# Scores of the new pair ahead of the old pair's transposes in a woven two-layer encoder

## The chip, the cores and the metric

The kernel runs on one core of a Trainium2 chip. The core has five engines with queues of their own: PE (TensorE, matrix products and transposes into PSUM), DVE (VectorE), ACT (ScalarE), POOL (GpSimd) and SP (SyncE, which issues the DMAs here). Each takes its instructions in the order of its queue, and they wait for one another by semaphores. The metric is device time in microseconds (us) of one execution, smaller is better.

## What is computed

A two-layer encoder trunk on 512 frames of 1024 channels, fp32, batch 1. Cut to what matters here:

```python
h = x
for layer in range(2):
    xn = rms_norm(h, norm_mix_g[layer])
    if layer == 0:   # A: sparse attention, each query keeps the top 128 admissible keys (rotary, 8 heads)
                     # B: chunked attention with a learned relative bias (8 heads)
        mix = even_mixer(xn, ...)
    else:            # C: forgetting attention (8 heads); D: windowed grouped attention with sinks (rotary, 8 heads)
        mix = odd_mixer(xn, ...)
    h = h + mix      # both mixers end in one output projection of their two head groups
    h = h + conv_gated_ffn(rms_norm(h, norm_ffn_g[layer]), ...)
return rms_norm(h, norm_out_g)
```

Every attention is: scores q.k, a bias or mask, softmax over the keys, product with v.

## The kernel before

**Precision.** Each fp32 operand is split into a high and a low part, and each product is three matmuls (`mm3`, L175 to 178): high with high, high with low, low with high. `hilo` (L182) makes such a pair from a result in PSUM: ACT copies the high part (L183), DVE subtracts to get the low part (L184). Weights come through a stream (`Stream`, L118): SP issues a DMA into `raw` (two buffers), ACT makes `whi` (L136), DVE or, for some, POOL makes `wlo` (L138); four buffers each.

**PSUM banks.** There are eight: two with the tag `acc` for projections, four with the tag `s` for scores, two with the tag `tp` for transposes, for the attention's output and for one narrow block of the scores (L97). A bank is taken in turn and can be filled again once its last reader is done.

**Weaves.** Attention is done for pairs of heads, one pair after another. A call of `weave(prev, cur, fill, n)` (L513) does the scores and the softmax of the new pair `cur` and, woven into them, the transposes, the product with v and the storing of the old pair `prev`. Between these steps stand `n` steps of filling, cut into seven parts by the percentages in `PARTS`. A step is one `yield` of a projection: one `mm3` of 512 columns, three matmuls. The filling is a queue of projections in a fixed order: in layer 0 the q and k of later B pairs, then `A1` and `A2` (q and k of the A pairs, four pieces of 128 frames each, 8 steps a piece), with `vA` between them, then `oB`, the half of the output projection that belongs to B (8 chunks of 4 steps). The lists `FILL_B`, `FILL_A`, `FILL_C`, `FILL_D` give the `n` of each weave. I call the weaves B0 to B3, A0 to A4, C0 to C3, D0 to D4; A4 has no new pair.

**The start of a weave** before the change, in the order of the code:

- T0, `prev.turn(0, 0)`: four transposes of the old pair's head 0 into one `tp` bank (L480), emptied by `hilo` into `PTh` and `PTl`.
- The score, `cur.score()`: 24 products (L442) of 64 rows and 128 to 512 columns, in a fixed order. The block of row 1 of head 0 goes into one `tp` bank with the first products, that of head 1 into another `tp` bank with the last three; the other blocks go into the four `s` banks.
- R0 and R1, `cur.soft(e, (1,))` for heads 0 and 1: DVE adds the bias to that row block and takes its minimum (L463, tile `nm`), which frees the `tp` bank; ACT exponentiates (L465), DVE inverts the sum (L467), POOL scales.
- T1, `prev.turn(0, 1)`: four more transposes into a `tp` bank; then the first part of the filling, then T2, `prev.turn(0, 2)`, two transposes, and the rest of the softmax of head 0.

Later in the weave the old pair's products with v go into a `tp` bank and are stored by ACT (L506) and DVE (L507, tile `Y`).

**Rotary transposes.** When a piece of `A1` or `A2` ends, `evac_A` (L716) applies the rotary (three products on DVE at L363, a sum on POOL at L365) and hands four transposes with their evacuations, `turn` at L724 (PE L727), to `later` (L154). `later.push(n, fn)` runs `fn` after `n` ticks; a tick falls at the end of every piece of a projection.

**The end.** In the second layer's MLP the last of the eight chunks of the down projection is done in two halves of 256 columns (L848): each begins with `lead_sums` (L858), which adds up over partitions the squares that POOL has gathered from the first seven chunks (L213), two tiny products (L861, four matmuls on PE), and goes on with 66 matmuls (22 `mm3`).

The queues' orders are not quite that of the code: a planner goes through the instructions by their place in the code, with durations of its own, and lets a later one go first where an earlier one is not ready by its reckoning. The order of the score's products among themselves is fixed (L445).

Of the kernel before, what the change touches and what calls it, by code (L numbers as in the profile page):

```python
# [22 lines left out]
NFF = DFF // 128  # L23
# [51 lines left out]
NI = 324  # L75
ND = 264
FILL_B = (8, 24, 24, 24, 24)
FILL_A = (20, 22, 18, 12, 11)
FILL_C = (6, 18, 16, 15, 12)
FILL_D = (10, 9, 9, 9, 8)  # L80
PARTS = (0, 20, 40, 50, 60, 72, 90, 100)
# [5 lines left out]
def trunk(ctx, tc, a, out):  # L87
# [11 lines left out]
    def bank(tag, shape=(128, 512)):  # L99
        return psum.tile(list(shape), F32, name=tag, tag=tag, bufs=banks[tag])  # L100
# [72 lines left out]
    later = Later()  # L173

    def mm3(o, lh, ll, rh, rl, start, stop):  # L175
        nc.tensor.matmul(o, lh, rh, start=start, stop=False)  # L176
        nc.tensor.matmul(o, lh, rl, start=False, stop=False)  # L177
        nc.tensor.matmul(o, ll, rh, start=False, stop=stop)  # L178
# [80 lines left out]
    class Fill:  # L259
# [16 lines left out]
        def run(self):  # L276
            while self.q:
                self.step(1)
# [234 lines left out]
    def weave(prev, cur, fill, n, mid=None, share=PARTS):  # L513
        cut = [n * p // 100 for p in share]
        parts = [b - a for a, b in zip(cut, cut[1:])]
        if prev is not None:
            prev.turn(0, 0)
        if cur is not None:
            cur.score()
            for e in range(2):  # L520
                cur.begin(e)
                cur.soft(e, (1,))
        if prev is not None:
            prev.turn(0, 1)
        if cur is not None and cur.early:
            for e in range(2):
                cur.rest(e)
                cur.soft(e, (2, 0, 3))
        fill.step(parts[0])
        if prev is not None:  # L530
            prev.turn(0, 2)
        if cur is not None and not cur.early:
            cur.rest(0)
            cur.soft(0, (2, 0, 3))
        if prev is not None:
            prev.av(0, 0)
        fill.step(parts[1])
        if prev is not None:
            prev.av(0, 1)
            prev.store(0)  # L540
        if mid is not None:
            mid(0)
        fill.step(parts[2])
        if prev is not None:
            prev.turn(1, 0)
        fill.step(parts[3])
        if prev is not None:
            prev.turn(1, 1)
        fill.step(parts[4])
        if prev is not None:  # L550
            prev.turn(1, 2)
        if cur is not None and not cur.early:
            cur.rest(1)
            cur.soft(1, (2, 0, 3))
        if prev is not None:
            prev.av(1, 0)
        if mid is not None:
            mid(1)
        fill.step(parts[5])
        if prev is not None:  # L560
            prev.av(1, 1)
            prev.store(1)
        fill.step(parts[6])
# [41 lines left out]
    with ExitStack() as st:  # L605
# [110 lines left out]
        def evac_A(half):  # L716
            def f(t, o):
                if t == 0:
                    for p in range(2):
                        qkA[2 * half + p] = mp.tile([128, 2, 2, SEQ], F32R, name="qk", tag="qk", bufs=3)  # L720
                qr = sp.tile([128, 8, HD], F32, name="scr2", tag="scr2", bufs=2)
                rope(o.rearrange("p (a d) -> p a d", a=8), t, slice(0, 2), qr, 8)

                def turn():  # L724
                    pt = bank("tp", (128, 2, 2, 128))
                    for b in range(4):
                        nc.tensor.transpose(pt[:, b // 2, b % 2, :],  # L727
                                            qr[:, 2 * b:2 * b + 2].rearrange("p a d -> p (a d)"), ident)
                    for p in range(2):
                        qk = qkA[2 * half + p]  # L730
                        ts_ = slice(t * 128, (t + 1) * 128)
                        hilo(qk[:, 0, :, ts_], qk[:, 1, :, ts_], pt[:, :, p, :])
                later.push(1, turn)
            return f

        for f in chan_pair(mp, ("qB", 0), ("kB", 0), pairs[0]):
# [28 lines left out]
        for p in range(4):  # L765
# [4 lines left out]
            cur = Pair(mp, job, 2)  # L770
            weave(pend, cur, fill, FILL_A[p])
            if p == 0:
# [3 lines left out]
            pend = cur  # L776
        fill.add(out_half("oA", lambda k: pairs[4 + k]["y"], after=lambda c: absorb(c, 1), lead=(0, 1, 2)))
        weave(pend, None, fill, FILL_A[4])
        fill.run()

    def ffn(layer, after):
        with ExitStack() as st:
            fp = st.enter_context(tc.tile_pool(name=f"ffn{layer}", bufs=1))
            cw = fp.tile([128, 192], F32, name="cw")[:, :4 * NC_FF].rearrange("p (a b) -> p a b", b=4)
            nc.sync.dma_start(cw, a["conv"][layer])
            act = [fp.tile([128, 2, SEQ], F32R, name=f"act{j}") for j in range(NFF)]

            def conv(o, c, dst):
                v = fp.tile([128, SEQ], F32, name="ov", tag="ov", bufs=2)
                nc.vector.tensor_tensor(v, o, R, OP.mult)  # L790
                nc.scalar.activation(dst, v, AF.Identity, scale=cw[:, c, 2:3], bias=cw[:, c, 3:4])
                nc.vector.scalar_tensor_tensor(dst[:, 1:], v[:, :SEQ - 1], cw[:, c, 1:2], dst[:, 1:],
                                               op0=OP.mult, op1=OP.add)
                nc.vector.scalar_tensor_tensor(dst[:, 2:], v[:, :SEQ - 2], cw[:, c, 0:1], dst[:, 2:],
                                               op0=OP.mult, op1=OP.add)

            def up(key):
                W.ahead(2)
                ws = W.get(key, 128)
                o = bank("acc" if key[0] == "g" else "s")  # L800
                run(chan_mm(o, ws))
                return o

            def first_two():
                W.ahead(2)
                os_ = bank("acc"), bank("s")
                gens = [chan_mm(o, W.get((x, layer, 0), 128)) for x, o in zip("gu", os_)]
                for gen in gens:
                    for _ in range(KD - 2):
                        next(gen)  # L810
                for gen in gens:
                    run(gen)
                return os_

            for j in range(NFF):
                tmp = sp.tile([128, 2, SEQ], F32, name="scr", tag="scr")
                if j == 0:
                    g, u = first_two()
                    token_roots()
                    roots()  # L820
                else:
                    g = up(("g", layer, j))
                conv(g, j, tmp[:, 0])
                nc.scalar.activation(tmp[:, 0], tmp[:, 0], AF.Silu)
                if j > 0:
                    u = up(("u", layer, j))
                conv(u, NFF + j, tmp[:, 1])
                nc.vector.tensor_tensor(tmp[:, 0], tmp[:, 0], tmp[:, 1], OP.mult)  # L828
                hilo(act[j][:, 0], act[j][:, 1], tmp[:, 0])
            hold = [None]  # L830

            def weights(c, k):
                n = c * NFF + k
                if n % 8 == 0:
                    W.ahead(2)
                    hold[0] = W.get(("w", layer, n // 8), 128)
                return [x[:, n % 8, :] for x in hold[0]]

            for c in range(KD - 1 if layer else KD):
                o = bank("acc")  # L840
                for k in range(NFF):
                    wh, wl = weights(c, k)
                    mm3(o, wh, wl, act[k][:, 0], act[k][:, 1], k == 0, k == NFF - 1)
                add_resid(c, o)
                after(c, slice(0, SEQ))
            if layer:
                ws = [weights(KD - 1, k) for k in range(NFF)]
                for cols in (slice(0, 256), slice(256, 512)):  # L848
                    o = bank("acc")
                    lead_sums(cols)  # L850
                    for k in range(NFF):
                        mm3(o[:, cols], *ws[k], act[k][:, 0, cols], act[k][:, 1, cols], k == 0, k == NFF - 1)
                    add_resid(KD - 1, o, cols)
                    after(KD - 1, cols)
# [3 lines left out]
    def lead_sums(cols):  # L858
        pt = sums["t"] = bank("tp", (128, NT))
        for t in range(cols.start // 128, cols.stop // 128):  # L860
            nc.tensor.matmul(pt[:, t:t + 1], hold_ss["t"][:, t * 128:(t + 1) * 128], ones[:, 0:1],  # L861
                             start=t * 128 == cols.start, stop=False)
# [401 lines left out]
```

## Time and profile before

| | |
|---|---|
| median of 3 runs | 1233.71 us (1233.11 to 1233.74) |
| the profiled execution | 1234.3 us, span 1232.4 us |
| mean granted clock of PE | 0.996 |
| busy | PE 98%, DVE 66%, ACT 48%, POOL 16% of the span |

The span runs from the first to the last instruction; some 1.9 us lie around it. PE's busy time is the union of its matmuls' modelled durations, so 98% does not mean that PE is at its peak. Rows name a line of the program (L480), the tile written and the tiles read (`tp<-ident,P`), partitions by elements, and how many instructions are merged (x4).

### The profile page before, as it was taken

The numbers are of one execution on the slowest core, as the hardware profiler recorded it, in microseconds if no ns is written. First come the engines' busy times: TensorE is split into PE (matmuls) and PEld (weight loads), VectorE is DVE, ScalarE is ACT, GpSimd is POOL, SyncE is SP. The second block draws the span as 40 slices with busy tenths as digits, with TensorE's granted clock in tenths as the row PEclk, the third lists the DMA queues.
The fourth block names the chain that finished last, engine by engine and source line by source line (L and its number), as shares of the span: only waits on it lengthen the run. The fifth ranks groups of instructions, "written<-read, shape, count | busy, mean of one in ns | idle before, by whom it ended". The sixth has DMA issues, their size and how long they took to land.

```text
span 1232.4 us, 15886 instructions
## 1 busy us (share of the span) xinstructions
PE 1204.5 (98%) x5908; PEld 993.3 (81%) x5908; DVE 813.8 (66%) x1469; ACT 593.5 (48%) x1008; POOL 199.9 (16%) x275
## 2 busy tenths in 40 slices
PE   8999899999999999999999999999999999999997
PEld 7777788778888888888888878778888888888886
DVE  7988987778877777733325566897777777762222
ACT  6555565666444444432224577785544444442221
POOL 3365322212000000000111354322000000000000
PEclk9999999999999999999999999999999999999999
DMA  6232213313333233233222320122332333323321
GB/s 217 86 105 85 69 44 120 111 35 106 104 102 102 88 102 101 88 102 102 87 70 86 114 70 24 37 84 72 103 94 95 103 93 96 103 92 96 103 69 69
DMA packets 35373, 111.71 MB, mean 91 GB/s; under 512 B 4192, under 2 KB 6624, under 8 KB 35296
## 3 DMA queue, kind: packets, MB, share of 16 engines
q1 hardware_dynamic: 35296, 110.70, 28.7%
q8 instruction: 46, 0.75, 0.3%
q14 instruction: 31, 0.25, 0.1%
HBM read 108.59 MB, written 2.10 MB: 90 GB/s over the span
## 4 chain that ended last, share of the span: by engine, by line
PE 80%; DVE 8%; ACT 4%; issue 4%; DMA 2%; POOL 1%; POOLq 0%; SPq 0%; DVEq 0%; ACTq 0%
PE acc L176 17%; PE acc L178 17%; PE acc L177 17%; PE s L176 8%; PE s L177 8%; PE s L178 8%; PE tp L480 1%; DMA raw<-in_w 1%; DVE wlo L138 1%; DVE wk L682 1%; ACT whi L136 1%; DVE P L463 1%; DVE m L681 1%; ACT P L465 1%; PE tp L497 1%
## 5 line engine op out<-in xcount | busy, mean ns | idle before, releaser
L138 DVE TENSOR_TENSOR wlo<-raw,whi 128x1024 fp32r<-128x1024 f32 (+2 forms) x188 | 237.0, 1261 | 159.8 <-ACT whi L136 156.9
L136 ACT ACTIVATE whi<-raw 128x1024 fp32r<-128x1024 f32 (+2 forms) x196 | 204.4, 1044 | 217.3 <-PE acc L177 144.5
L176 PE MATMUL acc<-xT,whi 128*128 128x512 f32 x480 | 189.2, 394 | 0.0
L178 PE MATMUL acc<-xT,wlo 128*128 128x512 f32 x480 | 187.0, 390 | 0.0
L177 PE MATMUL acc<-xT,whi 128*128 128x512 f32 x480 | 187.0, 390 | 0.0
L213 POOL TENSOR_TENSOR scr<-scr,os 128x512 f32<-128x512 f32 x24 | 34.5, 1439 | 722.2 <-ACT os L211 722.2
L176 PE MATMUL acc<-act,whi 128*128 128x512 f32 (+1 forms) x374 | 140.9, 377 | 0.0
L177 PE MATMUL acc<-act,whi 128*128 128x512 f32 (+1 forms) x374 | 140.9, 377 | 0.0
L178 PE MATMUL acc<-act,wlo 128*128 128x512 f32 (+1 forms) x374 | 140.9, 377 | 0.0
L176 PE MATMUL s<-xT,whi 128*128 128x512 f32 x352 | 136.9, 389 | 0.0
L177 PE MATMUL s<-xT,whi 128*128 128x512 f32 x352 | 136.9, 389 | 0.0
L178 PE MATMUL s<-xT,wlo 128*128 128x512 f32 x352 | 136.9, 389 | 0.0
L178 PEld LDWEIGHTS acc<-xT,wlo 128*128 128x128 f32 x480 | 90.2, 188 | 19.0
L176 PEld LDWEIGHTS acc<-xT,whi 128*128 128x128 f32 x480 | 90.1, 188 | 19.0 <-issue 1.0
L177 PEld LDWEIGHTS acc<-xT,whi 128*128 128x128 f32 x480 | 90.1, 188 | 18.6 <-issue 0.5
L176 PE MATMUL acc<-whi,xT 128*128 128x512 f32 (+2 forms) x208 | 84.5, 408 | 1.4 <-ACT whi L136 1.2
L177 PE MATMUL acc<-wlo,xT 128*128 128x512 f32 (+2 forms) x208 | 81.3, 392 | 1.1 <-DVE wlo L138 1.1
L178 PE MATMUL acc<-whi,xT 128*128 128x512 f32 (+2 forms) x208 | 81.3, 392 | 0.5 <-DVE xT L231 0.5
L176 PEld LDWEIGHTS acc<-act,whi 128*128 128x128 f32 x374 | 70.4, 188 | 13.0
L183 ACT ACTIVATE act<-scr 128x512 fp32r<-128x512 f32 x44 | 27.7, 630 | 110.2 <-DVE scr L828 110.2
L177 PEld LDWEIGHTS acc<-act,whi 128*128 128x128 f32 x374 | 70.4, 188 | 12.9
L178 PEld LDWEIGHTS acc<-act,wlo 128*128 128x128 f32 x374 | 70.4, 188 | 12.8
(244 smaller groups left out, 2174.5 us busy)
## 6 DMA issues: line engine op xcount, KB each, us to landing
raw<-in_w SPq DMA_DIRECT2D x188, 512.0 KB, 3.5
h<-in_x SPq DMA_DIRECT2D x16, 256.0 KB, 4.7
T<-in_relb SPq DMA_DIRECT2D x8, 256.0 KB, 2.8
raw<-in_w_i SPq DMA_DIRECT2D x4, 324.0 KB, 3.9
raw<-in_w_d SPq DMA_DIRECT2D x4, 264.0 KB, 2.8
out_y<-h SPq DMA_DIRECT2D x4, 256.0 KB, 2.2
out_y<-h SPq DMA_DIRECT2D x2, 384.0 KB, 2.4
ropeC<-in_ropeC SPq DMA_DIRECT2D x2, 256.0 KB, 4.1
```

The source lines that it names most:

```text
L136: nc.scalar.activation(hi[:, :w], raw[:, :w], AF.Copy)
L138: eng.tensor_tensor(lo[:, :w], raw[:, :w], hi[:, :w].bitcast(F32), OP.subtract)
L176: nc.tensor.matmul(o, lh, rh, start=start, stop=False)
L177: nc.tensor.matmul(o, lh, rl, start=False, stop=False)
L178: nc.tensor.matmul(o, ll, rh, start=False, stop=stop)
L183: nc.scalar.activation(dh, src, AF.Copy)
L213: eng.tensor_tensor(ss, ss, sq, OP.add)
L463: nc.vector.tensor_tensor_reduce(out=L, in0=self.s[e][i], in1=self.job["bias"][e][i], scale=1.0, scalar=3e38, op0=OP.add, op1=OP.min, accu ...
L465: nc.scalar.activation(L, L, AF.Exp, scale=-1.0, bias=nm, accum_out=sm)
L480: nc.tensor.transpose(pt[:, off:off + 128], self.L[e][i][:, j * 128:(j + 1) * 128], ident)
L497: nc.tensor.matmul(o[:, j * 128:512], v, th[:, off:off + w], start=j == 0, stop=False)
L681: tc.keep_in_program_order(nc.vector.max(m8, wk))
```

## The change

At the start of each weave the new pair's scores, with R0 and R1, stand in front of the old pair's T0; T1 follows T0. `FILL_A` is cut otherwise, with the same sum over the first four. The rotary transposes of `A1` wait two ticks in place of one (`half` is 0 for `A1`, 1 for `A2`). In the last chunk `lead_sums` is called in the middle of each half's loop, in place of ahead of it.

```diff
-FILL_A = (20, 22, 18, 12, 11)
+FILL_A = (22, 28, 12, 10, 11)
...
     def weave(prev, cur, fill, n, mid=None, share=PARTS):
         cut = [n * p // 100 for p in share]
         parts = [b - a for a, b in zip(cut, cut[1:])]
-        if prev is not None:
-            prev.turn(0, 0)
         if cur is not None:
             cur.score()
             for e in range(2):
                 cur.begin(e)
                 cur.soft(e, (1,))
         if prev is not None:
+            prev.turn(0, 0)
             prev.turn(0, 1)
...
-                later.push(1, turn)
+                later.push(2 - half, turn)
...
                     o = bank("acc")
-                    lead_sums(cols)
                     for k in range(NFF):
+                        if k == NFF // 2:
+                            lead_sums(cols)
                         mm3(o[:, cols], *ws[k], act[k][:, 0, cols], act[k][:, 1, cols], k == 0, k == NFF - 1)
```

## Rows read from the trace of the kernel before

**Rows 1.** The page, part 1: busy time, share of span, instructions of each engine.

```profile
PE 1204.5 (98%) x5908; PEld 993.3 (81%) x5908; DVE 813.8 (66%) x1469; ACT 593.5 (48%) x1008; POOL 199.9 (16%) x275
```

**Rows 2.** PE's waits, whole run: us in total, times, longest us.

```profile
PE tp L442 <- DVE PTl L184: 3.0, 3, 1.2
PE tp L727 <- DVE nm L463: 2.2, 1, 2.2
PE tp L480 <- DVE nm L463: 2.0, 3, 1.1
PE acc L176 <- DVE scr L363: 1.8, 2, 0.9
PE tp L442 <- DVE nm L463: 1.3, 1, 1.3
...
PE tp L861 <- POOL scr L213: 0.8, 1, 0.8
```

**Rows 3.** Windows by weave (B3, A3): length, busy us per engine, clock, DMA.

```profile
141.85:171.39 29.54, 26.50 (x141) 21.67 (x140) 26.95 (x66) 14.91 (x34) 7.40 (x10) 0.94 0.24 74
...
241.30:257.25 15.95, 15.89 (x97) 13.00 (x96) 12.30 (x32) 9.61 (x24) 4.26 (x7) 1.00 0.22 67
```

**Rows 4.** PE in order of time, B3's start: start, us, shape [idle before <-releaser].

```profile
141.85 0.60 PE L480 MATMUL tp<-ident,P 128*128 128x128 f32 x4
...
144.27 0.38 PE L442 MATMUL tp<-qk 64*128 64x256 f32 x1 [0.19 <-DVE Y L507]
...
147.12 0.66 PE L480 MATMUL tp<-ident,P 128*128 128x128 f32 x4 [0.66 <-DVE nm L463]
...
151.13 0.66 PE L727 MATMUL tp<-ident,scr 128*128 128x128 f32 x4 [2.19 <-DVE nm L463]
...
152.65 0.63 PE L177 MATMUL acc<-wlo,xT 128*128 128x512 f32 x1
```

**Rows 5.** DVE in order of time, B3's start.

```profile
149.33 1.41 DVE L138 TENSOR_TENSOR wlo<-raw,whi 128x1024 fp32r<-128x1024 f32 x1
150.66 0.41 DVE L463 CUSTOM_DVE_ANT_0 P<-tp,T 128x256 f32<-128x256 f32 x1
```

**Rows 6.** PE in order of time, A3's start.

```profile
241.30 0.60 PE L480 MATMUL tp<-ident,P 128*128 128x128 f32 x4
241.91 0.38 PE L442 MATMUL tp<-qk 64*128 64x256 f32 x1
...
244.03 0.66 PE L480 MATMUL tp<-ident,P 128*128 128x128 f32 x4
244.44 0.48 PE L176 MATMUL acc<-yT,whi 128*128 128x512 f32 x1
...
245.22 0.39 PE L176 MATMUL acc<-yT,whi 128*128 128x512 f32 x1
...
245.90 0.38 PE L480 MATMUL tp<-ident,P 128*128 128x128 f32 x2
```

**Rows 7.** DVE in order of time, A3's start.

```profile
242.63 0.69 DVE L184 TENSOR_TENSOR PTl<-tp,PTh 128x512 fp32r<-128x512 f32 x1
243.24 0.41 DVE L463 CUSTOM_DVE_ANT_0 P<-tp,wk 128x256 f32<-128x256 f32 x1
...
244.41 0.40 DVE L463 CUSTOM_DVE_ANT_0 P<-tp,wk 128x256 f32<-128x256 f32 x1
```

**Rows 8.** DVE and PE in order of time, C1's start.

```profile
715.73 1.21 DVE L138 TENSOR_TENSOR wlo<-raw,whi 128x1024 fp32r<-128x1024 f32 x1
...
717.60 0.38 PE L442 MATMUL tp<-qk 64*128 64x256 f32 x1 [1.22 <-DVE PTl L184]
```

**Rows 9.** All engines in order of time, the last chunk's first half.

```profile
1204.06 0.28 PE L176 MATMUL acc<-act,whi 128*128 128x256 f32 x1
...
1205.75 1.27 POOL L213 TENSOR_TENSOR scr<-scr,os 128x512 f32<-128x512 f32 x1 [13.67 <-ACT os L211]
...
1205.97 0.28 PE L177 MATMUL acc<-act,whi 128*128 128x256 f32 x1
```

## What I predict, and why

> **What bounds the kernel now.** I read the page's busy times first: PE has work in 98% of the span [rows 1], so time is gained only where PE waits, idles between steps or runs slow; all its idle time together is 1232.4 - 1204.5 = 27.9 us. Second, PE's own waits over the whole run [rows 2]. The reader is to see that most of them are on `tp` banks and end with a DVE instruction: the last score product of a weave (L442) waiting for the low half of T0 (PTl) or a reduction (nm), the second packet T1 and the third (L480) waiting for a reduction, one rotary transpose (L727) waiting 2.2 us, one matmul (L176) waiting 0.9 us for a rope, and at the very end L861 waiting 0.8 us for POOL. Third, weave by weave [rows 3]: B3 (141.85 to 171.39) has PE idle for 3.0 of 29.5 us and a granted clock of 0.94, and A3 with its 12 steps of filling has almost none. Fourth, PE and DVE in order of time at single starts of weaves [rows 4 to 8], to see which instruction of DVE's queue is late.
>
> **The start of a weave, moved.** Nothing is added or removed: 4 transposes and their two evacuations go behind 24 products. What changes is who waits for which of the two `tp` banks. Today T0 takes the bank that is free, the score's first product takes the one that head 1's attention output of the previous weave leaves (at B3 it waits for that, Y at L507 [rows 4]), its last three products take T0's bank again once ACT and DVE have emptied it, and T1 waits for the first reduction R0 (L463, head 0). Afterwards the score finds its first bank free and needs the second only at its end; T0 waits for R0, T1 for R1 (head 1), and R1 cannot begin before the last product. Whatever stands behind a waiting transpose on PE, the filling, waits with it; but the written order is not quite the queue's: at B3 seven filling matmuls stand between T0 and the score (141.85 to 144.27) [rows 4], so a planner fills expected gaps, and only lateness it did not foresee costs time.
>
> An undisturbed start, A3 [rows 6, 7]: T0 at 241.30, score 241.91, T1 244.03, filling 244.44. Moved, the score begins at about 241.4 and ends 0.5 us earlier, at about 243.6 (T1 began right behind it); R0 no longer stands behind PTl; T0 runs 243.6 to 244.0; R1 (0.4 us [rows 7]) runs from about 243.8 to 244.2, if the signal to DVE takes 0.2 (an estimate; no row here shows it alone); T1 at 244.25, filling at 244.65, which is 0.2 later than now. With filling between T0 and T1 it is 0. Four starts are like this (A0, A1, A3, C3): 0 to +0.8, I take **+0.4**.
>
> Four starts wait in the score's last products: 1.3 us in B1 (the one wait on nm), and 3.0 in the three on PTl (B2, C1 1.2, C2) [rows 2], 4.3 in all. At C1 the late thing is a split of weights, wlo, at 715.73 for 1.21 us, in front of PTl [rows 8]. The same wlo will then stand in front of R0 if the queue keeps its order, so T0 waits instead; R0 is shorter than PTl by some 0.3 us (0.41 against 0.69 in A3, [rows 7]). If the planner moves R0 ahead of it, most of the wait goes. Bounds: all 4.3 gone, or +0.3 each because R1 is exposed as well. With the same backlog in front I stay near the small end, 0.3 each: **-1.2**.
>
> B3 is the costly start. PE waits about 0.7 us for R0 (one of the three L480 waits, 2.0 less 1.1 and 0.3 elsewhere), then 2.2 us at the rotary transpose for R1, which runs only at 150.66, behind a wlo of 1.41 us [rows 5]; then the clock falls to its 1.2 GHz level: matmuls of 512 columns take 0.63 us [rows 4], against 0.39 in A3 [rows 6], and 0.06 of 29.54 us is 1.8 us lost [rows 3]. Together 4.7. After the change the score need not wait for Y and can start some 1.6 us sooner (seven matmuls of 0.23, a third of a step [rows 6]), so that R0 and R1 are ready before that wlo rather than after it. Against it, the rotary move does less than its name. With two ticks, the transposes of A1's t=0, 1, 2, 3 run at the ends of pieces t=2, t=3, vA 0, vA 1 instead of one piece earlier. At B3's start the end of t=3 still issues one (t=1's in place of t=2's), and its bank now waits for T0's low half; only its own data is surely ready. Its evacuations (two of 256 columns on ACT and two on DVE) are moved into a weave where DVE is busy for 26.95 of 29.54 us [rows 3]. No DMA moves with it. Bounds: 0, as DVE is the bound here, and -4.7; I take under half, **-2.0**, since DVE's late instructions change places but none goes away.
>
> **The filling of the A weaves.** 72 steps before and after in the first four, so PE's work is the same; eight steps of `oB` (two of A0, six of A1, at 0.68 us, three matmuls from 245.22 to 245.90 [rows 6]) come forward from A2 (18 to 12) and A3 (12 to 10). Their weights' DMAs and splits come forward too, in the same order in SP's queue, behind A2's weights; the eight reloads of `h` keep their place after A0. Now A2's score needs transposes of the piece that ended two steps before. Around that start PE waits 0.9 us for a rope to leave the acc bank and 1.1 us for R1 (the longest of L480's waits) [rows 2]. With ten steps of `oB`, 6.8 us, behind that piece, rope and rotary have run before A2 begins: the 0.9 should go, the 1.1 stands behind a wlo and may come back. Bounds 0 and -2.0, taken **-1.2**. In return A2 gets 12 steps, as A3 has now without a wait [rows 3], so no cost; A3 with 10 loses 1.4 us of cover. Bounds 0 and +2.8 (A2 paying as much); nearest is A3's row, so **+0.4**.
>
> **The end.** The first half of the last chunk starts at 1204.06 and PE stops after the matmul at 1205.97 for L861, which waits 0.8 us for POOL's addition of squares, 1205.75 to 1207.02 [rows 2, 9]. Put at k = 11 it stands behind 33 matmuls of 0.12 us (the 17th begins 1.91 us after the first), so at 1208.0, 1.0 us after POOL is done: the wait goes and everything behind it moves up. The second half's sums wait for nothing either way. **-0.9**, bounds -0.8 and -1.0; this is the surest term. In the D weaves the unit's score uses no `tp` bank, so the swap only reorders: 0, within 0.9 either way (their longest wait is the second L176 on a rope [rows 2]).
>
> **Sum.** +0.4 - 1.2 - 2.0 - 1.2 + 0.4 - 0.9 = -4.5 us. The profiled execution took 1234.3 us (span 1232.4, 1.9 around it), so 1229.8; it is 0.6 above the median of 1233.71, so for a median I say 1229.2.
>
> **Rivals.**
> *The waits only change their names.* DVE is 91% busy in B3; T0 waits for R0 behind the same splits, T1 for R1, and -1.2, -2.0 and -1.2 shrink to nothing together. For it: DVE ends almost every wait [rows 2]. Against it: in A2 and at the end the edit brings cover, not another order. The end alone remains: 1232.8.
>
> *Slower: R1 becomes the wait.* T1 goes into the bank that the score's last product has just filled, so PE stands still for R1: 0.2 of signal and 0.47 from R1's start to the transpose it releases (150.66 to 151.13) [rows 4, 5], less T0's 0.41 (as of T1, 244.03 to 244.44) [rows 6], 0.3 at six starts (A0, A1, A2, A3, B3, C3), and where a wlo of 1.2 us gets in front of R1 [rows 8], 1.2 at two of the other four: 1.8 + 2.4 - 0.9 = +3.3, 1237.0. It decides once new waits exceed 3.4 us with the old ones undiminished. For it: every weave has that chain; against it: the planner puts filling in such gaps [rows 4]. The Trainium skill speaks for this one (Perfetto Trace Analysis, Matmuls): independent groups of matmuls should rotate through PSUM banks, so that emptying one overlaps the next group's work. T1 behind the score does the opposite; by that rule this rival's time would come, and the trace agrees in so far as the waits of today are of that kind, on banks being emptied.
>
> *All listed waits go*: 0.9 + 4.7 + 2.0 + 4.3 = 11.9, 1221.8. Against it: DVE's work stays.
>
> **Chances.** Forecast 0.55 (own range 1226 to 1231.2), names only 0.24, R1 0.15, all gone 0.06. A difference under 0.2% (2.5 us) cannot be told from none here. So faster 0.61, same 0.24, slower 0.15. The range leaves out most of the last two cases: 1225.5 to 1235.5.
>
> **What would show it.** Right: L861 without a wait; no L442 wait on PTl; clock 1.00 through B3; no wait for a rope near the end of A1. Wrong: new L480 waits on nm of 0.3 us or more at most weaves; L727 waiting on PTl in B3; PE idle for over 1 us in A3 or A4. The forecast fails if the planner's new order puts other DVE work in front of R0 and R1, which no row of before can show.

## The result

The changed kernel is slower: 1241.07 us (median of six executions, 1238.96 to 1244.75) against 1233.72 us before on the same chip, a ratio of 1.0058, 95% interval 1.0042 to 1.0073. I had predicted 1229.2 and a range up to 1235.5. What came is the rival "R1 becomes the wait", about twice as large as I had priced it.

The page of the changed kernel, part 1 (as [rows 1]), from an execution of 1241.8 us with a span of 1240.0:

```profile
PE 1207.6 (97%) x5908; PEld 995.6 (80%) x5908; DVE 814.9 (66%) x1469; ACT 592.8 (48%) x1008; POOL 196.5 (16%) x275
```

The same instructions in 7.6 us more span: PE's idle time went from 27.9 to 32.4 us, and its busy time rose by the other 3.1 us, in stretches of lowered clock shown below. PE's waits, whole run (as [rows 2]; us in total, times, longest):

```profile
PE tp L480 <- DVE nm L463: 13.0, 11, 2.4
...
PE tp L497 <- DVE qk L184: 1.1, 1, 1.1
...
PE acc L176 <- DVE scr L363: 0.9, 1, 0.9
PE tp L726 <- DVE PTl L184: 0.9, 1, 0.9
```

The score waits for PTl no more (3.0 before), nor for a reduction (1.3), and L861 no more for POOL (0.8). In their place transposes wait eleven times for a reduction, 13.0 us in place of 2.0. Four of these waits are T0's for R0 (3.2 us: B1 1.46, B2 0.84, A0 0.55, A2 0.35), about what the score's last products waited before in B1 and B2 (1.26 and 0.69). Seven are T1's for R1 (9.8 us: B1 1.24, B2 2.38, B3 1.53, A0 1.73, A2 0.28, C1 0.65, C2 2.04).

Where the time went is read weave by weave, from the first score product of one to that of the next. The windows below are restricted to L177, one matmul per step of filling: length, PE's busy time on that line, behind x the number of steps done in the stretch, then the granted clock (the mean share of PE's full speed), and the DMA's share and GB/s. First the kernel before (B1, B2, B3, A0, A1, A2 and, behind the dots, C2), then the changed one:

```profile
90.51:115.83 25.32, 9.40 (x24) 1.00 0.32 104
115.83:144.27 28.44, 10.23 (x26) 1.00 0.12 35
144.27:171.92 27.65, 9.18 (x22) 0.94 0.20 61
171.92:194.50 22.58, 7.94 (x20) 1.00 0.32 99
194.50:225.10 30.60, 10.98 (x28) 1.00 0.41 125
225.10:241.91 16.81, 4.80 (x12) 1.00 0.24 79
...
735.23:755.72 20.49, 6.43 (x16) 1.00 0.16 52
```

```profile
91.72:119.90 28.18, 10.24 (x24) 0.94 0.27 92
119.90:150.08 30.18, 10.56 (x24) 0.89 0.07 20
150.08:179.30 29.22, 9.89 (x24) 1.00 0.22 74
179.30:204.33 25.03, 8.89 (x22) 1.00 0.30 94
204.33:233.84 29.51, 11.19 (x28) 1.00 0.45 150
233.84:250.16 16.32, 4.82 (x12) 1.00 0.21 71
...
741.48:763.52 22.04, 6.56 (x15) 0.92 0.15 49
```

B1 to B3 do 72 steps in both and take 81.4 us before, 87.6 after: +6.2, the greater part of the loss. Ahead of them B1's score begins 1.2 us later, which is no matter of the change (below). A1 and A2, 40 steps in both, gain 1.6.

B2's start shows the mechanism. PE, then DVE, in order of time, in the changed kernel:

```profile
122.94 0.66 PE L480 MATMUL tp<-ident,P 128*128 128x128 f32 x4 [0.84 <-DVE nm L463]
123.35 0.48 PE L176 MATMUL acc<-whi,xT 128*128 128x512 f32 x1
126.21 1.11 PE L480 MATMUL tp<-ident,P 128*128 128x128 f32 x4 [2.38 <-DVE nm L463]
...
128.40 0.63 PE L177 MATMUL acc<-wlo,xT 128*128 128x512 f32 x1
128.83 0.63 PE L178 MATMUL acc<-whi,xT 128*128 128x512 f32 x1
```

```profile
122.46 0.41 DVE L463 CUSTOM_DVE_ANT_0 P<-tp,T 128x256 f32<-128x256 f32 x1
...
122.80 0.75 DVE L363 TENSOR_TENSOR scr<-acc,ropeS 128x256 f32<-128x256 f32 x2
...
123.63 0.67 DVE L680 MAX8 m<-wk 128x8 f32<-128x512 f32 x1
...
124.42 0.68 DVE L681 MATCH_REPLACE8 wk<-m,wk 128x512 f32<-128x512 f32 x1
125.13 0.69 DVE L680 MAX8 m<-wk 128x8 f32<-128x512 f32 x1
125.74 0.41 DVE L463 CUSTOM_DVE_ANT_0 P<-tp,T 128x256 f32<-128x256 f32 x1
```

T0 runs 0.48 us after R0's start, one filling matmul follows, and T1 stands 2.38 us for R1, which DVE runs 3.28 us after R0, behind rope and top-k work. Then 512-column matmuls begin every 0.43 us in place of 0.23: PE is at its 1.2 GHz level. And the same weave of the kernel before, DVE and PE:

```profile
118.35 0.41 DVE L463 CUSTOM_DVE_ANT_0 P<-tp,T 128x256 f32<-128x256 f32 x1
...
121.63 0.40 DVE L463 CUSTOM_DVE_ANT_0 P<-tp,T 128x256 f32<-128x256 f32 x1
```

```profile
119.03 0.66 PE L480 MATMUL tp<-ident,P 128*128 128x128 f32 x4
...
122.27 0.38 PE L480 MATMUL tp<-ident,P 128*128 128x128 f32 x2
```

R1 ran 3.28 us behind R0 there too, to the hundredth. But T1 (119.03) took the bank that R0 frees, and R1's bank went to T2 at 122.27, twelve filling matmuls later. Here the change did not make R1 late; it put a transpose where the lateness had been covered.

In C2 it is a split of weights, here of 2.29 us. DVE in the kernel before, then DVE and PE in the changed one:

```profile
735.82 1.21 DVE L138 TENSOR_TENSOR wlo<-raw,whi 128x1024 fp32r<-128x1024 f32 x1
...
738.15 0.41 DVE L463 CUSTOM_DVE_ANT_0 P<-tp,G 128x256 f32<-128x256 f32 x1
...
739.36 0.42 DVE L463 CUSTOM_DVE_ANT_0 P<-tp,G 128x256 f32<-128x256 f32 x1
```

```profile
742.83 0.41 DVE L463 CUSTOM_DVE_ANT_0 P<-tp,G 128x256 f32<-128x256 f32 x1
...
743.77 2.29 DVE L138 TENSOR_TENSOR wlo<-raw,whi 128x1024 fp32r<-128x1024 f32 x1
...
746.06 0.40 DVE L463 CUSTOM_DVE_ANT_0 P<-tp,G 128x256 f32<-128x256 f32 x1
```

```profile
746.53 1.11 PE L480 MATMUL tp<-ident,P 128*128 128x128 f32 x4 [2.04 <-DVE nm L463]
```

This lateness is new. Before, a split stood in front of both reductions and R1 followed R0 by 1.21 us; now R0 runs ahead of a split and R1 behind it, 3.23 us after R0.

At the end (as [rows 9]) L861 follows its neighbour without a wait, as expected:

```profile
1216.54 0.28 PE L178 MATMUL acc<-act,wlo 128*128 128x256 f32 x1
1216.66 0.50 PE L861 MATMUL tp<-ones,scr 128*128 128x1 f32 x4
```

### The profile page after: what moved, and what is told of

Same layout as the page of the kernel before. It is cut to its first block, busy times and chain, and to the rows that moved or that the text cites. A ratio compares the mean times of both kernels' runs of the same rounds, so it can differ in the third digit from the quotient of the medians.

```text
span 1240.0 us, 15887 instructions
## 1 busy us (share of the span) xinstructions
PE 1207.6 (97%) x5908; PEld 995.6 (80%) x5908; DVE 814.9 (66%) x1469; ACT 592.8 (48%) x1008; POOL 196.5 (16%) x275
## 4 chain that ended last, share of the span: by engine, by line
PE 81%; DVE 10%; ACT 4%; issue 2%; DMA 2%; POOL 1%; SPq 0%; DVEq 0%; ACTq 0%; POOLq 0%
PE acc L178 17%; PE acc L177 17%; PE acc L176 17%; PE s L176 7%; PE s L177 7%; PE s L178 7%; PE tp L480 2%; DVE wlo L138 2%; DMA raw<-in_w 1%; DVE wk L681 1%; DVE m L680 1%; PE tp L498 1%; PE tp L497 1%; ACT whi L136 1%; DMA h<-in_x 1%
## 5 line engine op out<-in xcount | busy, mean ns | idle before, releaser
L177 PE MATMUL acc<-xT,whi 128*128 128x512 f32 x480 | 188.5, 393 | 0.0
L177 PE MATMUL acc<-act,whi 128*128 128x512 f32 (+1 forms) x374 | 141.0, 377 | 0.0
L177 PE MATMUL s<-xT,whi 128*128 128x512 f32 x352 | 136.9, 389 | 0.0
L177 PEld LDWEIGHTS acc<-xT,whi 128*128 128x128 f32 x480 | 91.0, 190 | 18.8 <-issue 0.5
L177 PE MATMUL acc<-wlo,xT 128*128 128x512 f32 (+2 forms) x208 | 82.6, 398 | 0.6 <-DVE wlo L138 0.6
L176 PEld LDWEIGHTS acc<-act,whi 128*128 128x128 f32 x374 | 70.4, 188 | 13.0
L177 PEld LDWEIGHTS acc<-act,whi 128*128 128x128 f32 x374 | 70.4, 188 | 12.9
L178 PEld LDWEIGHTS acc<-act,wlo 128*128 128x128 f32 x374 | 70.4, 188 | 12.8
```

## The experiments

Theory R: T1 waits for R1. Rival F: the filling list and the rotary tick are the loss. Rival D: the old pair's chain begins later, and that is the loss. Each ratio is to the kernel before on the same chip, with its 95% interval; executions of one kernel spread over some 5 us, so verdicts go by these and not by one profile. Much of that spread lies ahead of B1: the score of B0 began between 70.4 and 73.5 us in the fourteen profiles, at 72.84 with the end edit alone, whose queue on PE is before's until then (70.44).

**The swap alone** (e1_swap_only).

```diff
-        if prev is not None:
-            prev.turn(0, 0)
         if cur is not None:
             cur.score()
...
         if prev is not None:
+            prev.turn(0, 0)
             prev.turn(0, 1)
```

> The kernel before with the swap in the weaves alone (old filling list, old rotary tick, lead_sums in its old place). Theory R (T1 takes the bank that the score has just filled and stands still for R1, which DVE runs only after top-k, rope or split work): the trace of after has 13 us of T1 waiting for R1 over 11 starts and two stretches with a lowered clock; without the gain at the end (1.06 us) and A2's (about 1.7) it should stand 8 to 10 us above before, 1242 to 1244. Rival F (the filling list and the rotary tick are the loss): within 2 us of before. Rival D (the old pair's chain T0 to the product with v begins later, and that is the loss, whatever T1 waits for): the same as R here.

Measured: 1241.35, ratio 1.0050 (1.0038 to 1.0063): 4.7 to 7.8 us above before, less than the 8 to 10 expected. As near as the intervals tell, the swap alone is as slow as the whole change; F falls. Its waits for reductions repeat those of the changed kernel (12.1 us; 0.80 and 2.38 in B2, 2.01 in C2).

**All but the swap** (e2_no_swap): the changed kernel with T0 ahead of the score again.

> The changed kernel with the old order in the weaves alone (new filling list, new rotary tick, lead_sums in the middle). Theory R: T1 has its own bank and is covered again, A2's cover and the end's gain stay: 1.0 to 2.7 us below before, about 1231 to 1232.7. Rival F: near the changed kernel, 1239 or more. Rival D: as R.

Measured: 1234.04, ratio 0.9993 (0.9983 to 1.0003), by the ratio 0.9 us below before, where 1.0 to 2.7 was expected. The swap costs 6 to 8 us (e1_swap_only against before, the changed kernel against this one, by the ratios); what is left is worth nothing that can be told from the whole time. Its waits for PTl are back, 3.5 us.

**The end alone** (e3_end_only).

```diff
-                    lead_sums(cols)
                     for k in range(NFF):
+                        if k == NFF // 2:
+                            lead_sums(cols)
```

> The kernel before with lead_sums in the middle of each half alone. All theories: the wait of L861 for POOL, 0.8 us, goes and with it 0.9 to 1.1 us: about 1232.7. If the tail of after was shorter for another reason, no change.

Measured: 1234.21, ratio 0.9986 (0.9976 to 0.9996): about 1.7 us, interval 0.5 to 3.0, which holds the 1 us foreseen.

**T0 behind the score, T1 covered** (e4_cover): the changed kernel, T1 moved in front of T2.

```diff
         if prev is not None:
             prev.turn(0, 0)
-            prev.turn(0, 1)
...
         fill.step(parts[0])
         if prev is not None:
+            prev.turn(0, 1)
             prev.turn(0, 2)
```

> The changed kernel with T1 moved behind the first part of the filling, directly in front of T2; T0 stays behind the score. Theory R: R1 now has the first part of the filling to come in, so T1's waits for R1 (13 us with T0's) fall below 4 us and the time to 1230 to 1234, about 8 below the changed kernel. Rival D: T1 and the product with v come still later, the time stays at 1240 or rises. Rival F: stays near 1241.

Measured: 1230.56, ratio 0.9965 (0.9952 to 0.9978): some 11 us below the changed kernel by the two ratios, and faster than before. Its waits of transposes for reductions:

```profile
PE tp L480 <- DVE nm L463: 3.8, 5, 1.5
```

Four of these five are T0's for R0; T1 waits for R1 only in C2, 0.2 us. D falls: T1 comes later still and the time drops.

**The old order with T1 covered** (e5_old_t1_late): T0 ahead of the score, T1 moved as in e4_cover.

> e2_no_swap (old order, T0 ahead of the score) with T1 moved behind the first part of the filling as in e4_cover. It asks which half of e4_cover gives its gain. If T1's cover alone: like e4_cover, about 1230.5. If the place of T0 (the score's last products no longer wait for PTl, 3.5 us in e2_no_swap, and no transposes stand in front of the score): like e2_no_swap, about 1234, with L442 still waiting 3 us or more for PTl. Theory R takes the second.

Measured: 1236.08, ratio 1.0002 (0.9992 to 1.0013). Its waits:

```profile
PE tp L442 <- DVE PTl L184: 4.5, 5, 1.2
PE tp L480 <- DVE nm L463: 2.7, 1, 2.7
```

The cover alone gains nothing: in the old order T1 had little to wait for. So putting T0 behind the score was a sound idea in itself, and putting T1 right behind T0 spoilt it.

**Less top-k work on DVE** (e7_new_1round, e8_old_1round): one round of the selection in place of sixteen, in the new order and in the old.

```diff
-            for r in range(TOPK // 8):
+            for r in range(1):
```

> The changed kernel with one round of the top-k selection in place of sixteen (the selection is left out but for its first round). Theory R says that in B1 and B2 R1 is late because MAX8, MATCH and rope work runs on DVE between R0 and R1: B1's and B2's four waits for reductions (5.9 us in after) fall below 2.5 us, and the kernel stands only 2 to 4 us above e8_old_1round (C2's, A0's and B3's waits stay). A rival, R1 is late of itself because the score's last product ends only then: the same four waits stay, and 6 to 8 us above e8_old_1round.

> e2_no_swap (old order in the weaves) with one round of the top-k selection in place of sixteen (left out but for its first round), the partner of e7_new_1round. B1's wait of L442 for R0 (1.2 us) should go; 1 to 4 us below e2_no_swap, 1230 to 1233.

Measured: 1227.65 in the new order (ratio 0.9933, 0.9918 to 0.9949) and 1227.73 in the old (0.9932, 0.9917 to 0.9947). Without that work the swap costs nothing that can be told. The old order gained some 7.5 us by leaving it out, more than the 1 to 4 expected. B1 and B2 of the new order wait for no reduction at all; what is left is 3.3 in B3, behind two splits, C2 and three small ones. The waits of e7_new_1round, then DVE at its B2's start:

```profile
PE tp L480 <- DVE nm L463: 6.6, 5, 3.3
```

```profile
115.08 0.41 DVE L463 CUSTOM_DVE_ANT_0 P<-tp,T 128x256 f32<-128x256 f32 x1
...
116.29 0.42 DVE L463 CUSTOM_DVE_ANT_0 P<-tp,T 128x256 f32<-128x256 f32 x1
```

R1 comes 1.21 us behind R0 here, in place of 3.28. I had expected 2 to 4 us to remain, for B3, A0 and C2; but A0's waits went, and the old order has a wait to match B3's, 3.7 us of the rotary transpose for R1.

**R1 earlier** (e9_new_r1_first): the changed kernel, with head 1's block of row 1 at the start of the score.

```diff
-            for e, order in ((0, (1, 2, 0, 3)), (1, (2, 0, 3, 1))):
+            for e, order in ((0, (1, 2, 0, 3)), (1, (1, 2, 0, 3))):
```

> The changed kernel with the score's products in another order: head 1's block of row 1 comes at the start, beside head 0's, in place of at the end, so that R1 can run some 1.2 us earlier, while the rest of the score runs. T1 stays directly behind T0. Theory R (R1 comes late to T1): the waits of L480 for nm fall from 13 us to 3 to 7 us and the time to 1232 to 1237; where a wlo or a top-k instruction of over 1 us stands in front, part of the wait stays. Rival (T1's place itself, or the clock, is the loss): 1240 or more.

Measured: 1234.33, ratio 0.9986 (0.9976 to 0.9996), some 9 us below the changed kernel by the two ratios, with T1 in the same place:

```profile
PE tp L480 <- DVE nm L463: 4.3, 8, 1.3
```

**T0's transposes three times** (e6_t0_thrice): more work for PE in the gap ahead of T1, written to the same place.

```diff
+            for again in range(3 if (e, n) == (0, 0) else 1):
                 off = 0
                 at = {}
                 for j in pk:
```

> The changed kernel with T0's four transposes issued three times into the same place (same result, eight transposes of PE work more in each weave that has an old pair, about 0.8 us, some 13 us over 16 weaves with C and D in which T0 exists). It asks whether PE's idleness in front of T1 is the loss or only the lateness of what follows. Theory R with the waits as the whole loss: where PE waited 0.8 us or more for R1 (B1, B2, B3, A0, C2) the repeats lie in the wait and cost nothing; elsewhere they cost 0.8 each: the waits on nm fall from 13 to 8 us or less and the time rises by 4 to 9 us, 1245 to 1250. If the lowered clock that followed the waits (3 to 5 us of the loss in the profiled run) comes from PE's idle stretch, it returns to 1.00 in B1 and B2 and the time rises by less than 4 us.

Measured: 1242.04, ratio 1.0054 (1.0040 to 1.0069). T0 is so repeated in twelve weaves, not sixteen (the old pairs of D1 to D4 have a transpose of their own): 96 more matmuls at 0.10 us, 9.8 us of work, for 1 us more time, inside the spread. B2's start, and windows of B1 and B2 (length, busy us per engine, clock):

```profile
122.84 1.53 PE L481 MATMUL tp<-ident,P 128*128 128x128 f32 x12 [0.82 <-DVE nm L463]
126.11 0.65 PE L481 MATMUL tp<-ident,P 128*128 128x128 f32 x4 [1.74 <-DVE nm L463]
```

```profile
94.69:119.83 25.14, 24.60 (x142) 20.60 (x141) 18.57 (x53) 13.88 (x30) 16.32 (x18) 1.00 0.31 102
119.83:147.58 27.75, 25.19 (x145) 20.94 (x144) 23.76 (x61) 12.41 (x29) 8.66 (x14) 1.00 0.08 22
```

T1 starts when R1 lets it, with the repeats or without; the waits fall to 8.2 us in all, and the clock stays at 1.00 after both weaves. The mean granted clock was 0.996 to 0.998 in its six executions, 0.991 to 0.995 in those of the changed kernel, 0.989 to 0.994 with the swap alone. So the loss has two parts, standing still and running slow after it, and dead work in the gap gives the second back: of its 9.8 us 4.8 lie in the waits (13.0 to 8.2), and nearly all of the rest comes back. Less than 4 us more was expected of such a case, which came; the waits stayed just above the 8 us expected.

**Both cures together** (e10_cover_r1_first): e4_cover with the score order of e9_new_r1_first.

> e4_cover with the score order of e9_new_r1_first (head 1's block of row 1 at the start). If R1 is covered already by the first part of the filling, no more is to be had: as e4_cover, ratio 0.9965. If e4_cover's remaining waits on nm (3.8 us at L480, 1.3 at L726) come from R1's late start, up to 3 us lower, 1227.5.

Measured: 1233.94, ratio 0.9992 (0.9981 to 1.0003): not lower, but above e4_cover. Its profiled execution, 1238.08, is the slowest of its twelve; it lies 4.5 us behind e4_cover's at B1's score already (94.62 and 90.16), is level from there to A2 and loses 3.6 more from A2's score to the end. Why its median is higher stays open.

**The covered swap without the filling and rotary moves** (e11_cover_old_fill).

> e4_cover with the old filling list and the old rotary tick, so the covered swap and the end alone. If the filling and rotary moves are worth the 1 to 2 us that A2's waits suggested: ratio to before 0.9975 to 0.998. If they are worth nothing, as e2_no_swap beside e3_end_only suggests: 0.9965 as e4_cover.

Measured: 1229.47, ratio 0.9958 (0.9945 to 0.9970): those moves are worth nothing that the whole time shows in this order either.

**The same, D weaves in the old order** (e12_cover_abc).

```diff
+        old = share is PARTS_D or (cur is not None and cur.early)
+        if prev is not None and old:
+            prev.turn(0, 0)
         if cur is not None:
             cur.score()
...
         if prev is not None:
-            prev.turn(0, 0)
+            prev.turn(0, int(old))
...
         if prev is not None:
-            prev.turn(0, 1)
+            if not old:
+                prev.turn(0, 1)
             prev.turn(0, 2)
```

> e11_cover_old_fill with the D weaves (and D0, whose old pair is of C) back in the old order; A, B and C weaves keep T0 behind the score and T1 behind the first part of the filling. In the profiled runs the stretch from C3's score to the second MLP took 115.4 us in e11_cover_old_fill, 114.1 in the changed kernel and 113.3 in before. If the covered swap loses those 2.2 us in D: ratio to before 0.994, about 2 us below e11_cover_old_fill. If the 2.2 us are a matter of the filling there, not of T0 and T1: 0.9958 again.

Measured: 1228.46 against 1236.32, ratio 0.9935 (0.9921 to 0.9948): the fastest version that leaves no work out. Its stretch of D (748.83 to 863.52) took 114.7 us, so 0.8 of the 2.2 came back, and 0.7 of the 2.2 are a step of filling more in that stretch (117 in both versions, 116 in before); the intervals of this and e11_cover_old_fill overlap, and the step between them is not settled. PE at B2's start:

```profile
118.45 0.65 PE L480 MATMUL tp<-ident,P 128*128 128x128 f32 x4 [0.69 <-DVE nm L463]
...
121.72 0.66 PE L480 MATMUL tp<-ident,P 128*128 128x128 f32 x4
122.99 0.44 PE L480 MATMUL tp<-ident,P 128*128 128x128 f32 x2 [0.61 <-DVE PTl L184]
```

T1 follows T0 by 3.27 us, with twelve filling matmuls between, and waits for nothing.

## Why the prediction was wrong

| term | forecast, us | profile, us | how it is read |
|---|---|---|---|
| undisturbed starts A0, A1, A3, C3 | +0.4 | +2.0 | A0's waits 0.32 to 0.55 + 1.73; A1, A3, C3 none |
| B1, B2, C1, C2 | -1.2 | +7.2 | lengths: B1 +2.9; B2 +1.7 and two steps fewer (1.4); C1 -1.0; C2 +1.6 and one step fewer (0.7) |
| B3 | -2.0 | +0.2 | 27.65 to 29.22 with two steps more (1.4) |
| A2 and its filling | -0.8 | -1.6 | A1 and A2 together, 47.41 to 45.83 |
| the end | -0.9 | -1.06 | from the second MLP's first instruction (869.00, 877.66) to the span's end |

They sum to +6.7; 1.2 us ahead of B1 and -0.3 elsewhere complete the span's 7.6. Each measured value is from one execution of either kernel.

**The step that failed** is the second term, with the rival's price behind it. I let B1, B2, C1 and C2 gain 0.3 us each, because R0 is shorter than PTl, and kept R1's exposure as a bound of 0.3 each; the rival priced it at 0.3, or 1.2 behind a split, from A3 (a reduction that comes promptly) and from one split of 1.2 us. The runs showed T1 waiting 9.8 us for R1, 6.3 of them in these four starts. For the B weaves and A0, how late R1 is stood in the trace of before: its start less R0's is 2.71 us in B1, 3.28 in B2, 4.0 in B3 and 2.06 in A0, against 1.17 in A3. T1 begins 0.47 after R1 starts, T0 0.48 after R0, so a T1 directly behind T0 must wait for about that distance less T0's 0.41 and less the filling between: in B2 3.28 - 0.41 - 0.48 = 2.4, and 2.38 came; in B1 1.8, and 1.24 came, as R1 ran 2.12 after R0 there. I looked for the waits that there were, and not for the late instructions whose lateness nobody felt. C2 could not be read so: its distance was 1.21, and the new order put a split between its reductions. That is the condition of failure in my last sentence, which I gave no price.

The same wait is what made the first term wrong: A0, counted as undisturbed, already had a T1 waiting 0.32 us and an R1 2.06 behind R0. The signal of 0.2 us to DVE, given without a row, was not the mistake: in C0 of the kernel before, the products that fill R0's bank end by the profile at 699.41 and R0 begins at 699.56.

**The planner's filling.** I counted on it to put filling into the gap, as at B3 [rows 4]. Between T0 and T1 it put one matmul in B1, B2, C1, C2 and A1 to A3, two in A0 and four in B3. That its durations let R1 look prompt would explain it; no run looked into the planner.

**The clock.** The lowered stretch of B3 [rows 3] did go, as forecast, and came back larger in B1, B2 and C2: 0.06 of 28.18, 0.11 of 30.18 and 0.08 of 22.04, 6.8 us against 1.8 by the prediction's way of reckoning. That way counts too much: with the same instructions PE's busy time rose by 3.1 us, not 5.0. No term of mine held a clock that falls elsewhere.

**B3.** Its two waits of 2.85 became three of 2.77 (0.37 for Y, 1.53 for R1, 0.87 of the rotary transpose for PTl). R0 and R1 did not get ahead: with top-k, rope and a low half (`yT`) between them R1 ran 3.20 us after R0. My lower bound, 0, was the right value.

**The filling list** was costed on a wrong picture. In before, A1 did 28 steps and A2 12 (the windows above): the planner had already pulled forward what `FILL_A` assigned to A2. The new list writes down nearly that. So A2 was no longer the weave with 18 steps that I costed. In place the term still came out: with the new list the wait for a rope near the end of A1 (0.90 us at 220.41 before, 0.8 to 0.9 in e1_swap_only, e3_end_only and e11_cover_old_fill) is gone, and in three pairs of profiles A1 and A2 together are 0.7 to 1.3 us shorter with it (45.8 us in the changed kernel, 46.9 in e1_swap_only). That this lies near the -0.8 forecast, with a wrong count of steps behind it, is in part luck; and in the whole time the pairs of kernels with and without these edits (e2_no_swap and e3_end_only, e4_cover and e11_cover_old_fill) cannot be told apart.

**What was right**: no wait on PTl in the score, clock 1.00 through B3, no wait for a rope near the end of A1, L861 without a wait and its 1 us, A3 unharmed, C1 shorter, and the rival's mechanism. Two of the signs set for being wrong came as well: waits of L480 for nm of 0.3 us or more, at seven starts, and the rotary transpose waiting for PTl in B3. The Trainium skill (Perfetto Trace Analysis, Matmuls) wants independent groups of matmuls to rotate through PSUM banks, so that emptying one overlaps the next group's work. This trace agrees: transposes waited 13.0 us for banks that a reduction had yet to empty, and 3.8 in e4_cover, which puts filling between.

## What to carry to other kernels

Before a consumer is moved up to a bank, read when that bank's last reader runs in every instance, and not only where PE waits for it today: its distance from the reader before it, less the work left between, is about the new wait, as long as the new order puts nothing else between the two readers. Lateness that a few matmuls cover shows in no list of waits. And look at how many steps a stretch really holds before a filling list is costed; a planner may have dealt them out otherwise.

## What the runs showed of the hardware

A wait cost more than its length. After PE had stood 0.84 and 2.38 us with 0.9 us of matmuls between, the next eleven filling matmuls of B2 came 0.43 us apart, at 1.2 GHz; with 1.74 us of standing and repeated transposes in the rest of the gap (e6_t0_thrice) they came 0.23 apart. It is not certain at every such wait: in e1_swap_only the same 2.38 us in B2 left the clock at 1.00 and B3 and A0 ran at 0.94 and 0.93. Also, one split of weights of the same shape took 1.21, 1.41 [rows 5, 8] and 2.29 us; the longest ran while POOL was subtracting for a `qk` (743.67, 1.31 us). In the changed kernel's trace 151 splits of that shape on DVE had no POOL instruction beside them for more than 0.3 us, and all took 1.21 to 1.23; every longer one had such a neighbour, though several with one took no longer. That POOL slowed them was not tried by an experiment.
